# Sums of the first down-projection operands, formed by adding DMA transfers in memory instead of on VectorE

## The chip, the cores and the metric

The kernel runs on one core of one Trainium2 chip. The metric is the device time of one execution in microseconds, taken as the median of three runs.

## The reference, cut to what matters

The program is one decoder layer in float32: a mixer of two parts, an output projection, and then the channel mixer, which is where the change lies. For 512 rows of width 2048 it computes

```
h    = rmsnorm(x, norm2_g)
up   = h @ ffn_w_up                       # 2048 -> 2 * 6144
up   = causal depthwise conv, width 3, over rows
gate, val = split(up, 2)
x    = x + (gelu(gate) * val) @ ffn_w_down   # 6144 -> 2048
out  = rmsnorm(x, final_g)
```

The product `gelu(gate) * val` (512 rows by 6144 channels) is the left operand of the down projection.

## The kernel before, in words

**Fast block products.** Both big matrices of the channel mixer are multiplied by a Winograd scheme: two matrices of 2 by 2 blocks are multiplied with seven block products instead of eight. Each operand then needs, beside its four blocks, sums of its blocks. A tile `q` of eight slots of 128x256 holds one operand: slots 4 to 7 its four blocks as loaded, slots 0 to 3 the sums. The tables `SLOTS` and `ORDER` say which slots the seven products take and in which order they run. Float32 precision comes from splitting each slot into a rounded part (a cast on ScalarE, `h`) and a rest (a subtraction on VectorE, `l`; both at L126 and L127), and each product is three matmuls.

**Units and blocks.** The work goes through a stream of items: weight tiles (`Weights`) and operand tiles (`Acts`). A unit is one weight tile against one operand: 42 matmuls of 128x256. There are 24 blocks of 8 units for the up projection (unit numbers `u` 0 to 191; 12 groups `g`, each a gate block and a `val` block), and then three chunks of the down projection (units from 192; chunk 0 takes operands 0 to 7). Each item goes through `load` (a DMA on SP's queue into one of three rotating `q` buffers, a buffer being free again once its split is done), `sums` (three VectorE instructions, L646 to L648 for weights, L672 to L674 for operands; nothing where the sums were made beforehand) and `pair` (the split). The function `prepare` puts them in this order on the engines: the sums of item n+1, then the split of item n. All three engines run a fixed order from there on.

**Block ends.** The seven products of a block stand in seven of the eight PSUM banks. After a block VectorE and ScalarE combine them (`combine`, L870 to L878 in up blocks, L971 to L978 in down blocks), and TensorE takes over one bank after another as they come free. Later, spread over the steps of the next block, the convolution (`tap`, `rest`), gelu, and for `val` blocks the product with the gate (L921) follow. The product is written to memory by a POOL DMA, into `ad[p]`, 128 rows by 4 slots of 256 columns (L923). It is read back as an operand (L666) when its chunk begins.

**Sums made beforehand.** For the units around the start of each chunk (units 184 to 199 for chunk 0) the sums of the weights are made in memory: a list `to_make` of POOL transfers copies blocks and adds others (`accum_op`), and `make(n, after)` issues the next n of them. With `after` given, a one-column copy into `pace` (L318) holds POOL back until the last split of weights is done, so the list is spread over the whole program. These weights come with two loads, the sums (L639, 512 KB) and three of the blocks (L640, 384 KB).

The operands of chunk 0 cannot be split ahead: their tiles are the same as those of the up projection, so operand i waits until unit 184+i has been multiplied. They stand in the stream after the weights of units 187, 188, 190, 191, 193, 194, 196 and 197.

Of the kernel before, what the change touches and what calls it, by code (L numbers as in the profile page):

```python
# [8 lines left out]
F32 = mybir.dt.float32  # L9
# [3 lines left out]
ALU = mybir.AluOpType  # L13

P = 128
# [31 lines left out]
CHUNKS = [range(0, 8), range(8, 16), range(16, 22)]  # L47
# [31 lines left out]
def hybrid_block(ctx: ExitStack, tc: tile.TileContext, x, xT, w_in, w_out, w_up, w_dn, w_m4, w_dl, wab, wsT, vec, bs, vgb, fg, out):  # L79
    nc = tc.nc  # L80
# [213 lines left out]
    made = {}  # L294
# [13 lines left out]
    to_make = []  # L308
# [3 lines left out]
                to_make += copies[n] if part == 0 else added[n][0] if part == 1 else [added[n][1][part - 2]]  # L312
    pace = const.tile([P, 1], F32, name="pace")

    def make(n, after=None):

        if after is not None:
            nc.gpsimd.tensor_copy(pace, after)  # L318
        for _ in range(min(n, len(to_make))):
            add, dst, src = to_make.pop(0)  # L320
            how = {"accum_op": ALU.add} if add else {}
            nc.gpsimd.dma_start(dst, src, max_dma_last_dim=8192, **how)  # L322

# [192 lines left out]
    for i in range(2):  # L516
        for st in range(NS):
            t = vv[i][:, st]
# [5 lines left out]
    for i in range(2):  # L524
        ps = project(w_in, B_U + i, xg, True)
        t = rp.tile([P, 4, S], F32, name="uu", tag="r")
# [78 lines left out]
    x2d = [tc.dram_tile([P, NS, 512], F32, name=f"x2d{d}") for d in range(4)]  # L605
    ad = [tc.dram_tile([P, 4, 256], F32, name=f"ad{i}") for i in range(NP)]

    def squares2(d):
        nc.gpsimd.dma_start(x2d[d], x2[d])
        for st in range(NS):  # L610
            sq = pools["t"].tile([P, S], F32, name="sq", tag="sq", bufs=2)
            nc.scalar.activation(sq, x2[d][:, st], AF.Square, accum_out=ss2[:, st, d:d + 1])
# [15 lines left out]
    class Weights:  # L628


        def __init__(self, src, made=None):
            self.src, self.made = src, made
# [9 lines left out]
        def sums(self):  # L642
            q = self.q
            if self.made is not None:
                return
            nc.vector.tensor_tensor(q[:, 2:4], q[:, 5:7], q[:, 7:8].broadcast_to([P, 2, 256]), ALU.add)  # L646
            nc.vector.tensor_tensor(q[:, 1], q[:, 2], q[:, 6], ALU.add)
            nc.vector.tensor_tensor(q[:, 0], q[:, 1], q[:, 4], ALU.add)  # L648
# [8 lines left out]
    class Acts:  # L657


        def __init__(self, m, src=None, fill=None):  # L660
            self.m, self.src, self.fill = m, src, fill

        def load(self):
            self.q = slots("q")
            if self.fill is None:
                nc.sync.dma_start(self.q[:, 4:8], self.src)  # L666
            else:
                self.fill(self.q)

        def sums(self):  # L670
            q = self.q
            nc.vector.tensor_tensor(q[:, 2:4], q[:, 7:8].broadcast_to([P, 2, 256]), q[:, 5:7], ALU.subtract)  # L672
            nc.vector.tensor_tensor(q[:, 1], q[:, 6], q[:, 2], ALU.subtract)
            nc.vector.tensor_tensor(q[:, 0], q[:, 4], q[:, 1], ALU.subtract)  # L674
# [34 lines left out]
    def rest_of_loads():  # L709
        while halves:  # L710
            halves.pop(0)()
# [54 lines left out]
    spread = (0, 1, 3, 4, 6, 7, 9, 10)  # L766
    after = {}
    for m in range(8):
        after.setdefault(max(2, m), []).append(Acts(m, fill=from_rows(m)))
    for c, s in zip(CHUNKS, starts):  # L770
        for i, p in enumerate(c):
            after.setdefault(s - 8 + spread[i] + 3, []).append(Acts(i, src=ad[p]))

    def half_tiles(d):
        if d < 3:
# [82 lines left out]
    def later(step, f):  # L858
        lazy.setdefault(step, []).append(f)
# [22 lines left out]
    def up_block(g, val, u0):  # L882
        q = {}
        for m in range(8):
            prepare(ready(u0 + m))
            for p in ORDER:
                product(q, p, act[m], stream[place[u0 + m]].hl, True, m == 0, m == 7)
                if p == 6:
                    rest_of_loads()
            make(len(to_make) - n_make + n_make * (u0 + m + 1) // (n_up - 16), latest[0][:, 0, 0:1].bitcast(F32))  # L890
            if m == 7 and u0 == 0:
                pads[:] = [t_tile(f"pad{n}", [P, 2, S + 2]) for n in range(2)]
                for t in pads:
                    nc.gpsimd.memset(t[:, :, 0:2], 0.0)
            for f in lazy.pop(u0 + m, ()):
                f()
        c1 = t_tile("c1", [P, 2, 256])
        lo, hi = slice(2, 258), slice(258, 514)
        combine(q, c1, pads[0][:, :, lo], pads[1][:, :, lo], pads[0][:, :, hi], pads[1][:, :, hi])
        if u0 == 0:  # L900
            pools["ps"].release()
            pools["tr"].release()
            pools["ps"] = psum("q1", 8)

        def tap(n, j, f):
            if val:
                dst = t_tile("cv", [P, 2, S])if j == 0 else cvs[n]
                cvs[n] = dst
            else:
                if j == 0:  # L910
                    gates[n] = t_tile("gate", [P, 2, S], 2)
                dst = gates[n]
            nc.scalar.activation(dst[:, j], pads[n][:, j, 2:2 + S], AF.Identity, bias=col(V_FB + f), scale=col(V_FW + 2 * 96 + f))

        def rest(n, j, f):
            dst = (cvs if val else gates)[n][:, j]
            for i in (1, 0):
                nc.vector.scalar_tensor_tensor(dst, pads[n][:, j, i:i + S], col(V_FW + i * 96 + f), dst, ALU.mult, ALU.add)
            if val:
                gate = gates[n][:, j]  # L920
                nc.vector.tensor_tensor(gate, gate, dst, ALU.mult)  # L921
                at = 0 if j else 2
                nc.gpsimd.dma_start(ad[2 * g + n][:, at:at + 2], gate.rearrange("p (a b) -> p a b", a=2))  # L923

        def gelu(n, j):
            t = gates[n][:, j]
            nc.scalar.activation(t, t, AF.Gelu_apprx_tanh)

        cvs = {}
        at = u0 + 8  # L930
        for i, (n, j) in enumerate(((1, 0), (1, 1), (0, 0), (0, 1))):
            f = 48 * val + 4 * g + 2 * n + j
            step = at + (0, 1, 3, 4)[i]
            later(step, lambda n=n, j=j, f=f: tap(n, j, f))
            later(step + 1, lambda n=n, j=j, f=f: rest(n, j, f))
            if not val:
                later(step + 2, lambda n=n, j=j: gelu(n, j))

    pads = []
    for b, (g, val) in enumerate(ups):  # L940
# [6 lines left out]
    def down_block(ci, n, u0):  # L947
        tt = nc.vector.tensor_tensor
        size = len(CHUNKS[ci])
        q = {}  # L950
        for m in range(size):
            prepare(ready(u0 + m))
            if m == (6 if u0 == n_up else 1):
                if u0 == n_up:

                    pools["t"].release()
                    pools["x"] = pool("tx", "right")

            for half, at in ((0, 6 if u0 == n_up else 1), (1, 6 if u0 == n_up else 3)):
                if m == at:  # L960
                    t = pools["x"].tile([P, 2, 512], F32, name="xs", tag="xs", bufs=3)
                    nc.gpsimd.dma_start(t, x2d[n][:, 2 * half:2 * half + 2])
                    xs[n, half] = t
            for p in ORDER:
                product(q, p, act[m], stream[place[u0 + m]].hl, False, m == 0, m == size - 1)
            for f in lazy.pop(u0 + m, ()):
                f()
        X1, X2 = xs[n, 0], xs[n, 1]
        X11, X12, X21, X22 = X1[:, :, 0:256], X1[:, :, 256:512], X2[:, :, 0:256], X2[:, :, 256:512]
        c6, c5, c7 = (pools["x"].tile([P, 2, 256], F32, name="cc", tag="cc", bufs=3) for _ in range(3))  # L970
        tt(X11, X11, q[1], ALU.add)  # L971
        tt(X11, X11, q[2], ALU.add)  # L972
        nc.scalar.copy(c6, q[6])
        tt(c6, c6, q[1], ALU.subtract)
        nc.scalar.copy(c5, q[5])
        tt(X12, X12, q[3], ALU.add)
        nc.scalar.copy(c7, q[7])
        tt(X21, X21, q[4], ALU.add)  # L978
        steps = [
            lambda: tt(c5, c5, c6, ALU.add),  # L980
            lambda: tt(X12, X12, c5, ALU.add),
            lambda: tt(c6, c6, c7, ALU.add),
            lambda: tt(X21, X21, c6, ALU.subtract),
            lambda: tt(c5, c5, c7, ALU.add),
            lambda: tt(X22, X22, c5, ALU.add),
        ]
        if u0 + size == len(units):
            prepare(len(stream) - 2)
            for f in steps:
                f()  # L990
            prepare(len(stream) - 1)
            return
        at = u0 + size
        for i in range(3):
            later(at + i, steps[2 * i])
            later(at + i, steps[2 * i + 1])
        for half, t, step in ((0, X1, 0), (1, X2, 2)):
            later(at + step, lambda half=half, t=t: nc.gpsimd.dma_start(x2d[n][:, 2 * half:2 * half + 2], t))
# [6 lines left out]
    for n in DORD[:3]:  # L1005
        t = slots("q").rearrange("p a b -> p (a b)").rearrange("p (a b) -> p a b", a=NS)
# [116 lines left out]
```

## Time and profile before

| | us |
|---|---|
| median of 3 runs | 2063.87 (2063.66 to 2065.06) |
| the profiled execution | 2063.26 |
| its span in the trace | 2061.6 |
| TensorE busy | 2033.9 |
| VectorE busy | 1730.7 |
| ScalarE busy | 904.3 |
| POOL busy | 418.7 |

A row of groups names the line, the engine, the operation and its shapes, then the busy time, the mean duration in ns, and behind the second bar the idle time before these instructions with what ended it. A window row gives the busy time and the count of instructions of each engine in a stretch of time, then the granted TensorE clock (1.00 is full), the mean busy share of the 16 DMA engines and the GB/s moved. TensorE shows as busy for a matmul's whole modelled length, so a count of matmuls per stretch says more than its busy time.

### The profile page before, as it was taken

What the parts mean: (1) busy time and instruction counts of PE and PEld (TensorE: products, weight loads), DVE (VectorE), ACT (ScalarE), POOL (GpSimd) and SP (SyncE); (2) the same over time, 40 slices, a digit from 0 to 9 for tenths busy, and PEclk for the clock granted to TensorE, in tenths of its full rate; (3) what the DMA queues carried; (4) which work ended last, traced back from release to release, by engine and by line L of the source; (5) the groups of instructions that cost most, each with busy time, mean ns of one, the idle gap of its engine ahead of it and who ended that gap; (6) DMA issues with size and microseconds to landing.
All of it is one profiled execution on the core that took longest, in us unless ns stands there. A gap on an engine that the chain in (4) does not pass through costs nothing.

```text
span 2061.6 us, 35459 instructions
## 1 busy us (share of the span) xinstructions
PE 2033.9 (99%) x14528; PEld 1920.2 (93%) x14528; DVE 1730.7 (84%) x2183; ACT 904.3 (44%) x887; POOL 418.7 (20%) x702
## 2 busy tenths in 40 slices
PE   9999999999989999999999999999999999999998
PEld 7888888888889999999999999999999999999996
DVE  7598882644379999999999999999989979879986
ACT  6445322423274444444444444444455345445443
POOL 0332233211222222222222222222211000000001
PEclk9999999999999999999999999999999999999999
DMA  7666687666435566656555655565556568558573
GB/s 244 185 170 165 176 208 178 179 188 203 139 120 161 164 160 177 172 154 179 167 156 172 167 169 172 161 172 159 154 206 214 189 224 277 184 196 285 175 245 138
DMA packets 105907, 376.39 MB, mean 183 GB/s; under 512 B 14608, under 2 KB 22160, under 8 KB 91792
## 3 DMA queue, kind: packets, MB, share of 16 engines
q1 hardware_dynamic: 65808, 246.30, 35.5%
q0 software_dynamic: 39360, 127.17, 25.6%
q8 instruction: 113, 1.85, 0.4%
q10 hardware_dynamic: 576, 0.66, 0.1%
q14 instruction: 50, 0.41, 0.1%
HBM read 341.57 MB, written 110.36 MB: 219 GB/s over the span
## 4 chain that ended last, share of the span: by engine, by line
PE 93%; DVE 4%; DMA 1%; ACT 1%; issue 0%; SPq 0%; DVEq 0%; ACTq 0%
PE qs L854 64%; PE ps L162 9%; PE ps L164 9%; PE ps L163 9%; DVE wl L127 1%; DMA q<-ad 1%; PE qs L163 1%; PE qs L164 1%; PE qs L162 1%; DVE al L127 1%; PE tr L751 0%; PE ps L582 0%; ACT wh L126 0%; DVE q L672 0%; DMA wraw<-w_in 0%
## 5 line engine op out<-in xcount | busy, mean ns | idle before, releaser
L854 PE MATMUL qs<-ah,wh 128*128 128x256 f32 x2688 | 762.7, 284 | 2.1 <-DVE pad L871 1.8
L854 PE MATMUL qs<-al,wh 128*128 128x256 f32 x2688 | 761.5, 283 | 0.0
L854 PE MATMUL qs<-ah,wl 128*128 128x256 f32 x2688 | 761.5, 283 | 0.0
L126 ACT CAST wh<-q 128x1792 fp32r<-128x1792 f32 (+1 forms) x282 | 476.7, 1691 | 640.1 <-PE qs L854 459.6
L127 DVE TENSOR_TENSOR wl<-q,wh 128x1792 fp32r<-128x1792 f32 (+1 forms) x282 | 567.7, 2013 | 54.2 <-ACT wh L126 53.6
L854 PEld LDWEIGHTS qs<-ah,wh 128*128 128x128 f32 x2688 | 516.8, 192 | 2.5 <-DVE pad L871 2.0
L854 PEld LDWEIGHTS qs<-al,wh 128*128 128x128 f32 x2688 | 516.8, 192 | 0.2 <-DVE al L127 0.2
L854 PEld LDWEIGHTS qs<-ah,wl 128*128 128x128 f32 x2688 | 516.8, 192 | 0.0
L854 PE MATMUL qs<-wh,ah 128*128 128x256 f32 x1232 | 350.4, 284 | 5.7 <-DVE xs L972 2.6
L854 PE MATMUL qs<-wl,ah 128*128 128x256 f32 x1232 | 349.8, 284 | 0.0
L854 PE MATMUL qs<-wh,al 128*128 128x256 f32 x1232 | 349.7, 284 | 0.0
L318 POOL COPY pace<-wl 128x1 f32<-128x1 f32 x236 | 125.8, 533 | 975.5 <-DVE wl L127 965.5
L127 DVE TENSOR_TENSOR wl<-wraw,wh 128x1024 fp32r<-128x1024 f32 (+2 forms) x105 | 117.9, 1125 | 150.6 <-ACT wh L126 145.7
L854 PEld LDWEIGHTS qs<-wh,ah 128*128 128x128 f32 x1232 | 237.6, 193 | 6.9 <-DVE xs L972 3.0
L854 PEld LDWEIGHTS qs<-wl,ah 128*128 128x128 f32 x1232 | 237.6, 193 | 0.1
L854 PEld LDWEIGHTS qs<-wh,al 128*128 128x128 f32 x1232 | 237.6, 193 | 0.0
L322 POOL DMA_DIRECT2D made<-w_m x324 | 232.1, 842 | 15.8 <-issue 15.7
L126 ACT CAST wh<-wraw 128x1024 fp32r<-128x1024 f32 (+2 forms) x105 | 102.1, 974 | 274.6 <-PE ps L163 142.6
L646 DVE TENSOR_TENSOR q<-q 128x512 f32<-128x512 f32 x226 | 154.5, 684 | 2.7 <-DMA q<-w_dn 2.6
L162 PE MATMUL ps<-xgh,wh 128*128 128x512 f32 x384 | 152.1, 397 | 0.7 <-ACT wh L126 0.7
L163 PE MATMUL ps<-xgl,wh 128*128 128x512 f32 x384 | 151.6, 395 | 0.0
L164 PE MATMUL ps<-xgh,wl 128*128 128x512 f32 x384 | 150.0, 395 | 0.0
(242 smaller groups left out, 2499.4 us busy)
## 6 DMA issues: line engine op xcount, KB each, us to landing
q<-w_up SPq DMA_DIRECT2D x176, 512.0 KB, 3.5
made<-w_m POOLq DMA_DIRECT2D x270, 256.0 KB, 5.0
wraw<-w_in SPq DMA_DIRECT2D x28, 1024.0 KB, 6.1
q<-made SPq DMA_DIRECT2D x54, 512.0 KB, 3.7
q<-w_dn SPq DMA_DIRECT2D x50, 512.0 KB, 3.6
wraw<-w_out SPq DMA_DIRECT2D x16, 1024.0 KB, 6.1
q<-w_dn SPq DMA_DIRECT2D x38, 384.0 KB, 4.5
ad<-gate POOLq DMA_DIRECT2D x48, 256.0 KB, 3.5
```

Of the source, the lines that this page charges most:

```text
L126: nc.scalar.copy(h, src)
L127: nc.vector.tensor_tensor(l, src, h.bitcast(F32), ALU.subtract)
L162: nc.tensor.matmul(ps, lhsT=ah, rhs=bh, start=start, stop=False)
L163: nc.tensor.matmul(ps, lhsT=ah, rhs=bl, start=False, stop=False)
L164: nc.tensor.matmul(ps, lhsT=al, rhs=bh, start=False, stop=stop)
L318: nc.gpsimd.tensor_copy(pace, after)
L322: nc.gpsimd.dma_start(dst, src, max_dma_last_dim=8192, **how)
L646: nc.vector.tensor_tensor(q[:, 2:4], q[:, 5:7], q[:, 7:8].broadcast_to([P, 2, 256]), ALU.add)
L854: nc.tensor.matmul(q[p][:, t], lhsT=x_, rhs=y_, start=first and t == 0 and n == 0, stop=last and t == 1 and n == 2, skip_group_check=True)
```

## The change

It concerns the operands of chunk 0 alone. Their products are stored slot by slot (`ap[i]`, 4 slots of 128 rows by 256 columns), and in each of them two of the four quarter tiles with the opposite sign, so that all sums become plain additions. A second array `sums_of[i]` receives the four sums. They are made by five POOL transfers for each operand: two copies, then three that add. For these a slot is seen as 16 rows of 2048 elements (8 KB). One of the 40 transfers is issued at every second unit from unit 80 on (`make(1, todo=sum_up)`), with no pacing copy of its own. The operand is then loaded with two transfers (512 KB of sums, 384 KB of blocks) and has no sums on VectorE. The gate product is split into two halves of 256 columns, each with a factor of 1 or -1. In chunk 0 the combination after a down block subtracts where it added, since the products 2, 3, 5 and 7 now have the other sign.

```diff
@@ make @@
-    def make(n, after=None):
+    def make(n, after=None, todo=to_make):
...
-        for _ in range(min(n, len(to_make))):
-            add, dst, src = to_make.pop(0)
+        for _ in range(min(n, len(todo))):
+            add, dst, src = todo.pop(0)
@@ arrays in memory @@
+    ap, sums_of = ([tc.dram_tile([4, P, 256], F32, name=f"{n}{i}") for i in CHUNKS[0]] for n in ("ap", "as"))
+    for i in CHUNKS[0]:
+        ad[i] = ap[i].rearrange("s p c -> p s c")
@@ Acts.load, Acts.sums @@
+            if self.made is not None:
+                nc.sync.dma_start(self.q[:, 0:4], self.made.rearrange("s p c -> p s c"))
+                nc.sync.dma_start(self.q[:, 4:7], self.src[:, 0:3])
...
+            if self.made is not None:
+                return
@@ up_block @@
+            if u0 >= 80 and m % 2:
+                make(1, todo=sum_up)
             make(len(to_make) - n_make + n_make * (u0 + m + 1) // (n_up - 16), latest[0][:, 0, 0:1].bitcast(F32))
...
-                nc.vector.tensor_tensor(gate, gate, dst, ALU.mult)
+                if 2 * g + n in CHUNKS[0]:
+                    for t in (slice(0, 256), slice(256, 512)):
+                        nc.vector.scalar_tensor_tensor(gate[:, t], gate[:, t], -1.0 if (t.start == 0) == (j == 1) else 1.0, dst[:, t], ALU.mult, ALU.mult)
+                else:
+                    nc.vector.tensor_tensor(gate, gate, dst, ALU.mult)
@@ before the up blocks @@
+    sum_up = []
+    for k in range(len(CHUNKS[0]) + 3):
+        for r in range(4):
+            if 0 <= k - r < len(CHUNKS[0]):
+                dst, src = (t.rearrange("s (a b) c -> s a (b c)", b=8) for t in (sums_of[k - r], ap[k - r]))
+                sum_up += [
+                    [(0, dst[0:2], src[0:3:2]), (0, dst[2:4], src[1:3])],
+                    [(1, dst, src[3:4].broadcast_to([4, 16, 2048]))],
+                    [(1, dst[0:2], src[1:2].broadcast_to([2, 16, 2048]))],
+                    [(1, dst[0], src[2])],
+                ][r]
@@ down_block, likewise for X12, c5, c6 @@
+        plus = ALU.subtract if ci == 0 else ALU.add
-        tt(X11, X11, q[2], ALU.add)
+        tt(X11, X11, q[2], plus)
```

Three places show what moves. The first is POOL's queue around unit 93 in the difference of the two programs (`made` are the sums of weights, `as` the new sums, `ap` the slot-wise products; the shape is that of the transfer's list of rows, outermost count first).

```order
 L318 COPY pace<-wl 128x1
 L322 DMA made_596<-w_m 32x2048
+L322 DMA as_3713<-ap_3705 4x16x2048
 L318 COPY pace<-wl 128x1
 L322 DMA made_595<-w_m 32x2048
 L318 COPY pace<-wl 128x1
 L322 DMA made_595<-w_m 32x2048
+L322 DMA as_3715<-ap_3707 2x16x2048
 L318 COPY pace<-wl 128x1
 L322 DMA made_594<-w_m 128x512
```

A new transfer stands right behind a transfer of the old list, and the next `pace` copy behind it. Of the five for an operand three have an outermost count of 2 or 4 (one copy, two that add), the others 32 or 16 rows.

The second is VectorE's queue at the start of chunk 0 (units 186 to 188), before:

```order
L127 TENSOR_TENSOR wl<-q,wh 128x1792
L672 TENSOR_TENSOR q<-q 128x512
L673 TENSOR_TENSOR q<-q 128x256
L674 TENSOR_TENSOR q<-q 128x256
L127 TENSOR_TENSOR wl<-q,wh 128x1792
L127 TENSOR_TENSOR al_15210<-q,ah_15209 128x1792
L918 SCALAR_TENSOR_TENSOR gate<-pad_4967,vc,gate 128x512 x2
```

and now:

```order
L127 TENSOR_TENSOR wl<-q,wh 128x1792 x2
L127 TENSOR_TENSOR al_15280<-q,ah_15279 128x1792
L929 SCALAR_TENSOR_TENSOR gate<-pad_4983,vc,gate 128x512 x2
L127 TENSOR_TENSOR wl<-q,wh 128x1792
L127 TENSOR_TENSOR al_15340<-q,ah_15339 128x1792
```

The three sums of an operand are gone, so the split of the weights before it no longer stands behind the operand's load.

The third is SP's queue there, before:

```order
L666 DMA q<-ad_3682 128x1024
L639 DMA q<-made_569 128x1024
L640 DMA q<-w_up 128x768
L639 DMA q<-made_570 128x1024
L640 DMA q<-w_up 128x768
```

and now:

```order
L670 DMA q<-as_3714 128x4x256
L671 DMA q<-ap_3706 128x3x256
L643 DMA q<-made_569 128x1024
L644 DMA q<-w_up 128x768
L643 DMA q<-made_570 128x1024
```

An operand's load has become two transfers with rows of 1 KB in place of one with rows of 4 KB.

More of the change, by code (lines that the diff above doesn't have):

```diff
@@ L657, in hybrid_block, with __init__ @@
     class Acts:
-        def __init__(self, m, src=None, fill=None):
-            self.m, self.src, self.fill = m, src, fill
+        def __init__(self, m, src=None, fill=None, made=None):
+            self.m, self.src, self.fill, self.made = m, src, fill, made
         def load(self):
             self.q = slots("q")
-            if self.fill is None:
+            if self.made is not None:
+                nc.sync.dma_start(self.q[:, 0:4], self.made.rearrange("s p c -> p s c"))
+                nc.sync.dma_start(self.q[:, 4:7], self.src[:, 0:3])
+            elif self.fill is None:
                 nc.sync.dma_start(self.q[:, 4:8], self.src)
@@ L771, in hybrid_block @@
         for i, p in enumerate(c):
-            after.setdefault(s - 8 + spread[i] + 3, []).append(Acts(i, src=ad[p]))
+            after.setdefault(s - 8 + spread[i] + 3, []).append(Acts(i, src=ad[p], made=sums_of[i] if c is CHUNKS[0] else None))
     def half_tiles(d):
@@ L975, in down_block @@
         nc.scalar.copy(c5, q[5])
-        tt(X12, X12, q[3], ALU.add)
+        tt(X12, X12, q[3], plus)
         nc.scalar.copy(c7, q[7])
@@ L979, in down_block @@
         steps = [
-            lambda: tt(c5, c5, c6, ALU.add),
+            lambda: tt(c5, c6, c5, plus),
             lambda: tt(X12, X12, c5, ALU.add),
-            lambda: tt(c6, c6, c7, ALU.add),
+            lambda: tt(c6, c6, c7, plus),
             lambda: tt(X21, X21, c6, ALU.subtract),
-            lambda: tt(c5, c5, c7, ALU.add),
+            lambda: tt(c5, c5, c7, plus),
             lambda: tt(X22, X22, c5, ALU.add),
```

## The prediction

> **What bounds the kernel now.** I read the page first, then the groups and waits of TensorE, then the windows around unit 192, then VectorE's order in the up projection, and last the DMA queues.
>
> ```profile
> span 2061.6 us, 35459 instructions
> PE 2033.9 (99%) x14528; PEld 1920.2 (93%) x14528; DVE 1730.7 (84%) x2183; ACT 904.3 (44%) x887; POOL 418.7 (20%) x702
> ```
>
> TensorE bounds it. In the up projection (620 to 1510 us) it hardly ever waits, as the groups of its instructions there show:
>
> ```profile
> L854 PE MATMUL qs<-ah,wh 128*128 128x256 f32 x2465 | 697.8, 283 | 2.1 <-DVE pad L871 1.8 <-DVE v L877 0.3
> ```
>
> The windows around the start of chunk 0 show where it does wait (columns: stretch; PE, PEld, DVE, ACT, POOL; clock; DMA share; GB/s), and its timeline names the two waits:
>
> ```profile
> 1540.00:1550.00 10.00, 10.00 (x86) 10.00 (x85) 9.90 (x10) 6.99 (x6) 2.82 (x2) 1.00 0.53 186
> 1550.00:1560.00 10.00, 7.60 (x59) 7.40 (x59) 9.01 (x9) 6.38 (x6) 2.28 (x3) 0.92 0.68 244
> 1560.00:1570.00 10.00, 9.39 (x61) 9.09 (x61) 9.62 (x13) 3.60 (x4) 0.63 (x1) 0.74 0.40 141
> 1600.00:1610.00 10.00, 8.41 (x67) 7.90 (x67) 9.76 (x14) 4.86 (x5) 0.55 (x2) 1.00 0.83 291
> ...
> 1558.98 0.58 PE L854 MATMUL qs<-wh,ah 128*128 128x256 f32 x1 [2.40 <-ACT c L870]
> 1561.24 0.58 PE L854 MATMUL qs<-wh,ah 128*128 128x256 f32 x1 [0.61 <-DVE pad L871]
> ```
>
> Full pace is 85.5 recorded matmuls in 10 us. The three short windows lack 26.5 + 24.5 + 18.5 = 69.5, or 8.1 us. That is all there is to win here. About 3 us of it is no wait but a lower clock behind the wait (61 matmuls at a clock of 0.74 with only 0.61 us idle).
>
> The cause is VectorE: before the banks of the last up block are freed (L871) stand five operands' sums, and they wait for loads.
>
> ```profile
> 1518.92 2.02 DVE L127 TENSOR_TENSOR wl<-q,wh 128x1792 fp32r<-128x1792 f32 x1
> ...
> 1560.51 0.68 DVE L871 TENSOR_TENSOR pad<-c,qs 128x512 f32<-128x512 f32 x1
> ...
> L672 DVE TENSOR_TENSOR q<-q 128x512 f32<-128x512 f32 x8 | 5.5, 688 | 3.0 <-DMA q<-ad 3.0
> L674 DVE TENSOR_TENSOR q<-q 128x256 f32<-128x256 f32 x8 | 3.4, 425 | 0.3
> ```
>
> **What the change removes at chunk 0.** Per operand 0.69 + 0.43 + 0.43 = 1.54 us of VectorE, eight times 12.3 us. Five operands stand before L871: 7.7 us, and with the 3.0 us of waits at most 10.7 us. By VectorE alone L871 could start at 1550. The three `q` buffers allow less. A buffer's turn is the load, the cast, the split. An operand's load now looks like that of made weights, whose second transfer is issued 0.37 us after the first and lands as SP's rows say:
>
> ```profile
> 1509.26 0.33 SPq L639 DMA_DIRECT2D q<-made  x1
> 1509.63 0.43 SPq L640 DMA_DIRECT2D q<-w_up  x1
> ...
> DMA to landing us min/median/max: 4.0/4.2/5.4
> ...
> 1558.82 1.69 ACT L126 CAST wh<-q 128x1792 fp32r<-128x1792 f32 x1
> ```
>
> A turn is 0.4 + 4.2 + 1.7 + 2.0 + 0.2 for handing over = 8.5 us, with the longest landing 9.7; with the added traffic I take 9.0. From the split that ends at 1520.9 four turns lead to the split before L871: 1520.9 + 36 = 1556.9 instead of 1560.5. TensorE then waits about 1 us instead of 3.0, too little to expect the slow stretch (3 us); the wait of 1600 to 1610 (18.5 matmuls, 2.2 us) loses three more operands' sums, and I count half. Gain 2 + 3 + 1 = **6 us** (bounds 0 and 8.1).
>
> **Gate products.** Sixteen instructions of 128x512 become 32 of 128x256, in four `val` blocks.
>
> ```profile
> L921 DVE TENSOR_TENSOR gate<-gate,cv 128x512 f32<-128x512 f32 x20 | 13.8, 692 | 0.7
> L647 DVE TENSOR_TENSOR q<-q 128x256 f32<-128x256 f32 x79 | 33.6, 425 | 2.7
> L646 DVE TENSOR_TENSOR q<-q 128x512 f32<-128x512 f32 x79 | 54.0, 684 | 0.0
> L918 DVE SCALAR_TENSOR_TENSOR gate<-pad,vc,gate 128x512 f32<-128x512 f32 x40 | 29.9, 749 | 0.7
> ```
>
> Two at 0.425 are 0.16 us more than one at 0.692; with the 0.065 by which the scaled form is dearer at 512 columns (749 against 684) 0.29 us. Four of them in two blocks: 0.6 to 1.2 us. VectorE has just that much room, one wait of 1.19 us in every two blocks:
>
> ```profile
> DVE wl L127 <- ACT wh L126: 13.3, 11, 1.5
> ...
> 1031.17 0.68 DVE L871 TENSOR_TENSOR pad<-c,qs 128x512 f32<-128x512 f32 x1
> ...
> 1068.73 2.03 DVE L127 TENSOR_TENSOR wl<-q,wh 128x1792 fp32r<-128x1792 f32 x1 [1.19 <-ACT wh L126]
> ...
> 1111.80 0.68 DVE L871 TENSOR_TENSOR pad<-c,qs 128x512 f32<-128x512 f32 x1
> ```
>
> From L871 to L871 two blocks last 80.63 us. I count 0.5 us for all; without that cover it is 4 x 1.2 = 4.8.
>
> **The forty transfers.** POOL's groups from 1000 to 1400 us, and the landing of the old transfers:
>
> ```profile
> L322 POOL DMA_DIRECT2D made<-w_m x81 | 57.0, 711 | 4.1 <-issue 4.1
> L318 POOL COPY pace<-wl 128x1 f32<-128x1 f32 x79 | 39.5, 500 | 264.2 <-DVE wl L127 264.2
> ...
> made<-w_m POOLq DMA_DIRECT2D x270, 256.0 KB, 5.0
> ```
>
> On POOL the new ones cost nothing: 40 x 0.7 = 28 us of issue against 264 us in which `pace` waits for VectorE. Behind them in POOL's queue stand the next `pace` copy, the next old transfer and the stores of the gate products, for which nothing waits before the next chunk. What counts is the loads of weights beside them, since VectorE has 1.19 us to lose in 80. A load is issued when a split ends, lands 3.5 us later (row below, SP's L637 from 1000 to 1400 us), and its sums stand at a fixed place in VectorE's order:
>
> ```profile
> 1037.47 2.02 DVE L127 TENSOR_TENSOR wl<-q,wh 128x1792 fp32r<-128x1792 f32 x1
> ...
> 1044.31 0.69 DVE L646 TENSOR_TENSOR q<-q 128x512 f32<-128x512 f32 x1
> ...
> 1064.00 2.02 DVE L127 TENSOR_TENSOR wl<-q,wh 128x1792 fp32r<-128x1792 f32 x1
> ...
> 1075.45 0.68 DVE L646 TENSOR_TENSOR q<-q 128x512 f32<-128x512 f32 x1
> ...
> DMA to landing us min/median/max: 3.3/3.5/5.8
> ```
>
> In the first pair the split ends at 1039.4 and the sums of the load issued then begin at 1044.3: 4.9 us, 1.4 us of room. In the second it is 1065.9 to 1075.45, 9.5 us. Of the sixteen loads of two blocks four have 4.9 us, four 5.6, two 6.3 and six 7.8 to 9.5.
>
> The price of a row comes from the DMA view of two windows in which one old transfer of 32 rows of 8 KB runs (its 48 packets are 32 rows and 16 short marks): 1050 to 1053.2 us, an adding one, and 1063 to 1065, a copy (the first line is the first window in 40 slices, in tenths):
>
> ```profile
> DMA  6989796959892990009949400050559000000000
> q0 software_dynamic: 48, 0.26, 45.2%
> ...
> q0 software_dynamic: 47, 0.26, 31.9%
> ```
>
> 45.2% of 16 engines over 3.2 us is 23.1 us, 0.72 us for an added row; 31.9% over 2 us is 10.2 us, 0.33 for a copied one. At first all engines are busy (the digits of 9): the 32 rows are dealt two to an engine.
>
> How a transfer with an outermost count of 2 or 4 is dealt, no row shows; every one of before has 32 or 128. Bounds: by rows over 16 engines (4 added rows each for the 512 KB one), or by its outermost pieces over 4 or 2 engines, 16 rows each. The old ones fit both, as there a piece is a row. I take the pieces, 7 to 3, because they are what the transfer's list names first. [...]
>
> With pieces an adding transfer holds its engines 16 x 0.72 = 11.5 us. A load of 512 KB gives every engine 8 rows of 4 KB. If each waits behind one added row, it lands 8 x 0.72 = 5.8 us late, after 9.3 us. Against the room that is late by 4.4 (four loads), 3.7 (four), 3.0 (two) and about 0.8 (six), 2.7 in the mean. Loads come 3.4 to 8.2 us apart, so each adding transfer meets one nearly whole; but some of its rows have gone before the load comes, and 0.72 holds some waiting of its own. I take 2.0: 16 x 2.0 = 32 us. The eight uneven copies (8 x 0.33 = 2.6 us late) cost 1 us. Behind the late sums stand the split, the next sums and at a block's end the evacuation, and TensorE waits for that. VectorE gives back its 1.19 us in each of the five double blocks that the transfers span (40 x 10.1 us): 6 us, and evacuations can be 1 us late. Left are 32 + 1 - 6 - 1 = **26 us** (bounds 0, and 16 x 4.4 - 6 = 64).
>
> Each block's end in that stretch then has a wait of about 2.6 us, like the one of 2.40 above that brought a lower clock. A slowed TensorE lets VectorE catch up, so I count 2 us in all.
>
> **Sum.** The profiled execution took 2063.26, its span 2061.6; the runs' median is 2063.87, so the same. 2063.3 - 6 + 0.5 + 26 + 2 = **2086 us**.
>
> **Rivals.**
>
> *Spread over all engines, faster.* Then an adding transfer of 512 KB puts 4 rows, 2.9 us, on each engine, the others no more than the old ones do, beside which a load took up to 5.8 us and TensorE never waited. A load lands after 6.4 us, late by 1.5 for four in sixteen and 0.8 for four, 0.6 in the mean; eight of these, 4.8 us, are less than the 6 us given back. 2063.3 - 6 + 0.5 = 2058. It decides where a hit costs a load under about 2 us. For it: the digits of 9. Against: the outermost counts.
>
> *Spread, but the buffers take the gain, no change.* The operands' loads bring 384 KB more and rows of 1 KB into a stretch where DMA already stands at 0.68 to 0.83. If a turn takes 9.9 us, L871 comes at 1560.5 as now; only the 1 us of the later wait is left and the gate products take half: 2063.
>
> *Every wait slows the clock.* If each of ten block ends pays 3 us of lower clock, with nothing caught up, it is 2086 - 2 + 30 = 2114. For it: the clock of 0.74 after a wait of 2.4 us. [...]
>
> That the sums come too late for their loads I exclude: the last transfer stands near unit 160, the first load behind unit 185.
>
> **How the numbers follow.** The forecast has 0.62, the clock rival 0.08, the faster one 0.18, no change 0.12. About 0.2% (4 us) is what a measurement here can tell from no change: faster 0.18, same 0.12, slower 0.70. If pieces are right, the range by itself is 2068 to 2108 (a mean lateness of 0.9 to 3.4 us). To leave out no more than 2 in 10 it has to reach the faster case too: 2058 to 2108.
>
> **What would show it.** The transfers of 2x16x2048 and 4x16x2048 would land after 10 us and more, where the old ones took 5; loads of weights between 990 and 1400 us would land after up to 9 us; VectorE would wait there for q<-w_up, some 30 us in all; TensorE would wait at the ends of those ten blocks. From 1550 to 1610 us' counterpart the counts should be near 85. If the loads keep 3.5 us with a longest near 6, the step on the engines is wrong, and the time is near 2058.

## The result, and the profile after

The change makes the kernel slower: 2121.67 us median of four runs (2120.86 to 2123.78) against 2064.47 before, also of four (2063.66 to 2065.28), a ratio of 1.0280 with a 95% interval of 1.0267 to 1.0293. The profiled execution took 2123.78, its span 2122.1. That is 36 us over the forecast and 14 over the end of its range.

The page, then the DMA issues of the kernel after (size, median us from issue to landing), which answer to the 5.0 us of the old transfers and the 3.5 us of the loads:

```profile
span 2122.1 us, 35510 instructions
PE 2049.7 (97%) x14528; PEld 1930.8 (91%) x14528; DVE 1723.6 (81%) x2175; ACT 905.2 (43%) x887; POOL 443.7 (21%) x742
...
PE 71%; DVE 14%; DMA 11%; ACT 2%; issue 2%; SPq 0%; DVEq 0%; ACTq 0%
...
made<-w_m POOLq DMA_DIRECT2D x270, 256.0 KB, 5.1
...
as<-ap POOLq DMA_DIRECT2D x24, 256.0 KB, 10.0
...
as<-ap POOLq DMA_DIRECT2D x8, 512.0 KB, 16.1
```

VectorE is no longer busier, it has 7 us less work, and yet 14% of the chain of what ended last is its own and 11% is DMA. The new transfers take two to three times as long as the old ones of 256 KB (the 10.0 is the median of copies, of adds on two engines and of eight even copies). The waits of VectorE, of TensorE between 980 and 1580 us, and the loads of weights (SP's L641, 980 to 1480 us) tell the rest (columns of the waits: us in total, times, longest):

```profile
DVE q L650 <- DMA q<-w_up: 65.2, 21, 6.5
...
PE qs L863 <- DVE pad L880: 27.8, 9, 8.1
PE qs L863 <- DVE wl L127: 13.8, 8, 3.3
...
  DVE q L650: 64.9, 20
...
DMA to landing us min/median/max: 3.3/4.7/11.8
```

Where the time is lost is read from the evacuation that ends a block (L871 before, L880 after; L971 and L1002 in the first down block). Before:

```profile
990.03 0.68 DVE L871 TENSOR_TENSOR pad<-c,qs 128x512 f32<-128x512 f32 x1
...
1514.14 0.68 DVE L871 TENSOR_TENSOR pad<-c,qs 128x512 f32<-128x512 f32 x1
...
1605.48 0.68 DVE L971 TENSOR_TENSOR xs<-xs,qs 128x512 f32<-128x512 f32 x1
```

and after:

```profile
992.44 0.68 DVE L880 TENSOR_TENSOR pad<-c,qs 128x512 f32<-128x512 f32 x1
...
1576.98 0.68 DVE L880 TENSOR_TENSOR pad<-c,qs 128x512 f32<-128x512 f32 x1
1621.66 0.68 DVE L880 TENSOR_TENSOR pad<-c,qs 128x512 f32<-128x512 f32 x1
1664.27 0.69 DVE L1002 TENSOR_TENSOR xs<-xs,qs 128x512 f32<-128x512 f32 x1
```

The stretch in which the transfers are issued takes 584.54 us in place of 524.11, **60.4 us more**. The transition to chunk 0 behind it takes 87.29 in place of 91.34, **4.05 us less**. The difference of the spans, 60.5, is these two, 2.4 us that were there at 992 already, and 1.7 behind. The 2.4 us need not be the change's: the first evacuation of the up projection, ahead of all that the edits move, comes anywhere from 626.4 to 631.0 us in the traces of the kernels of this document.

VectorE's 64.9 us of waits for weights are 4.5 more than that: so much of its room it gave back, as I read it. TensorE pays partly in waits (41.6 us in the two rows above) and partly in a lower clock, as the windows of the kernel after show (columns as in the prediction):

```profile
640.00:1000.00 360.00, 360.00 (x3003) 360.00 (x3002) 345.17 (x452) 163.49 (x136) 95.12 (x159) 1.00 0.60 166
...
1100.00:1480.00 380.00, 342.27 (x2735) 338.52 (x2734) 318.74 (x402) 150.91 (x124) 109.97 (x180) 0.96 0.64 169
```

### The profile page after: what moved, and what is told of

Same layout as the page of the kernel before. It is cut to its first block, busy times and chain, and to the rows that moved or that the text cites. A ratio compares the mean times of both kernels' runs of the same rounds, so it can differ in the third digit from the quotient of the medians.

```text
span 2122.1 us, 35510 instructions
## 1 busy us (share of the span) xinstructions
PE 2049.7 (97%) x14528; PEld 1930.8 (91%) x14528; DVE 1723.6 (81%) x2175; ACT 905.2 (43%) x887; POOL 443.7 (21%) x742
## 4 chain that ended last, share of the span: by engine, by line
PE 71%; DVE 14%; DMA 11%; ACT 2%; issue 2%; SPq 0%; DVEq 0%; ACTq 0%
PE qs L863 42%; DMA q<-w_up 9%; PE ps L162 8%; PE ps L164 8%; PE ps L163 8%; DVE wl L127 7%; DVE q L650 2%; DVE q L651 1%; ACT wh L126 1%; DVE al L127 1%; PE qs L163 1%; PE qs L164 1%; PE qs L162 1%; DMA q<-w_dn 1%; DVE gate L929 1%
## 5 line engine op out<-in xcount | busy, mean ns | idle before, releaser
L318 POOL COPY pace<-wl 128x1 f32<-128x1 f32 x236 | 115.6, 490 | 1000.3 <-DVE wl L127 990.4
L650 DVE TENSOR_TENSOR q<-q 128x512 f32<-128x512 f32 x226 | 154.9, 685 | 67.8 <-DMA q<-w_up 65.2
```

## The experiments

The kernels were run in three sets, each on one chip beside the kernel before: e1 to e4 beside 2065.71 us (15 runs), e5 to e8 beside 2065.70 (21), e9 to e12 beside 2064.87 (21). "Waits" is VectorE's wait for `q<-w_up` in the profile; the last column is how long the 512 KB adding transfers took to land.

| run | transfers | us | ratio (95% interval) | waits, us | 512 KB lands, us |
|---|---|---|---|---|---|
| the change | 24 on few engines | 2121.67 | 1.0280 (1.0267 to 1.0293) | 65.2 | 16.1 |
| e1_spread | all spread | 2066.93 | 1.0005 (0.9996 to 1.0013) | 4.5 | 7.3 |
| e2_add4 | eight 512 KB adds on few | 2099.33 | 1.0166 (1.0150 to 1.0181) | 38.0 | 15.9 |
| e3_add2 | eight 256 KB adds on few | 2098.18 | 1.0157 (1.0144 to 1.0171) | 40.9 | 7.1 |
| e4_copy2 | eight copies on few | 2078.22 | 1.0060 (1.0046 to 1.0073) | 17.9 | 7.1 |
| e5_rows4k | as e2, rows of 4 KB | 2087.75 | 1.0109 (1.0093 to 1.0124) | 28.9 | 17.1 |
| e9_rows2k | as e2, rows of 2 KB | 2083.76 | 1.0091 (1.0077 to 1.0104) | 25.9 | 17.5 |
| e6_none | none | 2061.53 | 0.9981 (0.9972 to 0.9990) | 0.2 | |
| e8_transfers_only | all spread, unused | 2073.52 | 1.0043 (1.0030 to 1.0055) | 6.9 | 7.9 |
| e10_roomy_narrow | the change's, other units | 2101.34 | 1.0176 (1.0162 to 1.0189) | 37.8 | 15.5 |
| e7_roomy | all spread, other units | 2062.39 | 0.9984 (0.9975 to 0.9993) | 0.4 | 7.4 |
| e11_roomy_again | the same | 2061.59 | 0.9986 (0.9977 to 0.9995) | 1.1 | 7.2 |
| e12_spread_again | as e1 | 2066.87 | 1.0006 (0.9997 to 1.0015) | 5.5 | 7.2 |

### Is it the few engines?

Theory 1: the transfers with an outermost count of 2 or 4 lie on 2 or 4 engines, and the loads of weights wait there. The rival: 11.5 MB (8 x 1408 KB) more of traffic beside the loads costs it, however it is dealt. The edit puts the 16 rows outermost; by theory 1 the same rows of 8 KB then go over 16 engines:

```diff
-                dst, src = (t.rearrange("s (a b) c -> s a (b c)", b=8) for t in (sums_of[k - r], ap[k - r]))
+                dst, src = (t.rearrange("s (a b) c -> a s (b c)", b=8) for t in (sums_of[k - r], ap[k - r]))
...
-                    [(1, dst, src[3:4].broadcast_to([4, 16, 2048]))],
+                    [(1, dst, src[:, 3:4].broadcast_to([16, 4, 2048]))],
```

> The same forty transfers with the same bytes and the same 8 KB rows, but with the 16 rows of a slot outermost (16x4x2048 and 16x2x2048 instead of 4x16x2048 and 2x16x2048). Theory 1, few engines: the transfers of the changed kernel ran on 4 or 2 engines; now each puts 4 or 2 rows on all 16, lands after 5 to 7 us instead of 10 to 16, loads of weights land within 6.5 us, VectorE waits for q<-w_up at most 6 us in all (65.2 in the changed kernel), and the time is 2058 to 2062. Rival, the adding traffic itself (its bytes in memory, its issues on POOL): nothing changes, 2110 to 2122.

The DMA issues, VectorE's wait and the landing of the loads of weights in e1_spread:

```profile
as<-ap POOLq DMA_DIRECT2D x24, 256.0 KB, 5.4
...
as<-ap POOLq DMA_DIRECT2D x8, 512.0 KB, 7.3
...
DVE q L650 <- DMA q<-w_up: 4.5, 7, 1.1
...
DMA to landing us min/median/max: 3.4/3.6/8.6
```

2066.93 us, 5 above the range that I had expected, and the latest load landed after 8.6 us, not 6.5. But with the 16 rows outermost the 256 KB transfers land like the old ones (5.4 and 5.1 us), the 512 KB ones after 7.3 us in place of 16.1, and 55 of the 57 us are gone; the traffic is the same. The rival falls. How many engines an uneven transfer holds is seen in windows of the change in which only the added rows and the rows of a load are at work: behind a 512 KB adding transfer, from 1087.5 to 1090.7 us, both queues come to 4.0 engines (19.6% and 5.4% of 16), behind a 256 KB one, from 1323.1 to 1324.7 us, to 2.0 (9.8% and 2.7%). That the spread ones lie on all 16 is read from their landings; no window here counts them.

### Which transfers pay, and how much?

Here the two theories of the price are: (1a) each uneven transfer pays by itself, and the prediction's price was too low; (1b) two of them in flight at once pay for each other. Each run takes e1_spread and puts one kind alone back on few engines (for e2_add4 this is the line; the other two do the same with the adding `dst[0:2]` and with the copy `dst[:, 0:2]`):

```diff
-                    [(1, dst, src[:, 3:4].broadcast_to([16, 4, 2048]))],
+                    [(1, ndst, nsrc[3:4].broadcast_to([4, 16, 2048]))],
```

> Only the eight adding transfers of 512 KB keep their outermost count of 4; the other 32 have 16 or 32 outermost. In the changed kernel VectorE waited 64.9 us for loads of weights in this stretch, about 57 of it behind the sixteen uneven adding transfers, 3.6 each. Theory 1a, each transfer pays by itself and the forecast only had the price of one too low: 29 us of such waits here, 6 of them covered, 2082. Theory 1b, two uneven transfers in flight together make the price: 2.0 each as forecast, 16 us of waits, 2069.

> Only the eight adding transfers of 256 KB keep their outermost count of 2. They have as many rows per engine (16) as those of 512 KB, on half as many engines. Theory 1a: 29 us of waits, 2082, the same as with the 512 KB ones, since a load is as late as its latest engine. Theory 1b: 16 us, 2069. If the share of the engines counted and not the latest one, about half of what the 512 KB ones cost.

> Only the eight copies of 256 KB keep their outermost count of 2. A copied row took 0.33 us where an added one took 0.72. Theory 1a: 7 us of waits as behind these copies in the changed kernel (0.9 each), all but 1 covered by the room VectorE has: 2059 to 2062. Theory 1b: less than 7 us, the same time. If the price of a row did not matter, only that few engines are held: 29 us, 2082.

VectorE's wait in the three, in the order e2, e3, e4:

```profile
DVE q L650 <- DMA q<-w_up: 38.0, 11, 5.9
```

```profile
DVE q L650 <- DMA q<-w_up: 40.9, 16, 6.0
```

```profile
DVE q L650 <- DMA q<-w_up: 17.9, 12, 3.1
```

Alone, the 512 KB ones cost 38.0 / 8 = 4.75 us each, the 256 KB ones 5.1, the copies 2.2. e1_spread, where no transfer is uneven, has 4.5 us of such waits too; less these the copies cost 1.7. So 1b falls: each pays by itself, and more than the 3.6 of 1a (29 us and 2082 expected; 38.0 and 40.9 us, 2099.33 and 2098.18 measured). The 512 KB and the 256 KB ones, on 4.0 and 2.0 engines by the windows of the change, cost about the same, and in the change the 256 KB adding ones land after 14.1 to 15.9 us, the 512 KB ones after 15.0 to 17.0: what they share is 16 added rows on an engine, 32 over 2 and 64 over 4. That the latest engine decides is the reading of this, not more. The copies, too, cost more than 1a expected (17.9 us for 7). And the three do not add up: 96.8 us alone, in which those 4.5 us can stand three times, 65.2 together.

### How a load waits

The prediction let each of a load's eight rows on such an engine wait behind one added row, and one load pay for a transfer. A new theory then was that the load waits until the rest of the transfer has gone. Cutting the rows tells them apart, since the engine has about the same 10 us of rows to do, 16 x 0.63, 32 x 0.33 or 64 x 0.17 us by the windows below (e5_rows4k; e9_rows2k has 2048 and `[4, 64, 512]`):

```diff
-            nc.gpsimd.dma_start(dst, src, max_dma_last_dim=8192, **how)
+            nc.gpsimd.dma_start(dst, src, max_dma_last_dim=4096 if add == 2 else 8192, **how)
...
-                    [(1, ndst, nsrc[3:4].broadcast_to([4, 16, 2048]))],
+                    [(2, ndst, nsrc[3:4].broadcast_to([4, 32, 1024]))],
```

> The run with only the eight 512 KB adding transfers on few engines, again, but with their rows cut to 4 KB (four pieces of 32 rows instead of 16 rows of 8 KB). Theory of the prediction's working (a row of a load waits behind one row of the adding transfer at a time, by turns): a wait is half as long, so the loads of weights land at most about 8 to 9 us after their issue, VectorE waits about 15 us or less for them, and the time is near 2078 us. New theory (a load's rows on such an engine wait until most of what is left of the adding transfer's rows has gone): cutting the rows changes nothing but their number, the longest landing stays near 12 us, VectorE waits 35 to 45 us, and the time is 2095 to 2105 us.

> The eight 512 KB adding transfers on few engines once more, their rows cut to 2 KB (four pieces of 64 rows; an engine still has some 10 us of added rows to do). Theory now: on such an engine the rows of a load and of the adding transfer take turns one by one, and what a load is late by is handed to the next load on that engine if its rows are not done when that comes. With 2 KB rows a load's eight rows pass such an engine in about 8 x (0.16 + 0.16) = 2.6 us, less than the 5 us between loads, so nothing is handed on: a load lands about 1.3 us late, VectorE waits 5 to 14 us for weights, and the time is 2066 to 2074 us. If a load has to wait for most of the remaining rows, however short, VectorE waits 35 us and more and the time is near 2097. If only the sum of the added rows' time counts, it is that of the 4 KB rows: waits near 29 us, time near 2088.

The waits were 28.9 and 25.9 us, the times 2087.75 and 2083.76: in between, and both of my expectations for a theory alone missed. "Only the sum of the added rows' time counts" came nearest. The DMA view shows what happens on the engines while only these two queues are at work (POOL's q0 with the added rows, SP's q1 with the load's; packets, MB, share of 16 engines). In e5_rows4k, three half microseconds in a row from 1079.5 to 1081:

```profile
q0 software_dynamic: 4, 0.02, 16.4%
q1 hardware_dynamic: 4, 0.02, 8.7%
...
q0 software_dynamic: 4, 0.02, 16.4%
q1 hardware_dynamic: 4, 0.02, 8.7%
...
q0 software_dynamic: 4, 0.02, 16.4%
q1 hardware_dynamic: 4, 0.02, 8.7%
```

25.1% of 16 engines is 4.0 engines, and on each one added row of 0.33 us and one load row of 0.17 us pass per half microsecond: they take turns, one by one. With 8 KB rows (e2_add4, 1057 to 1061 us) and 2 KB rows (e9_rows2k, 1079.5 to 1081 us):

```profile
DMA packets 53, 0.26 MB, mean 65 GB/s; under 512 B 8, under 2 KB 8, under 8 KB 35
...
q0 software_dynamic: 26, 0.15, 17.8%
q1 hardware_dynamic: 27, 0.11, 7.1%
```

```profile
q0 software_dynamic: 20, 0.04, 14.0%
q1 hardware_dynamic: 17, 0.07, 12.3%
```

In e2 the 26 hold 8 short marks: 18 added rows of 0.63 us beside 27 load rows, again 4.0 engines. In e9 20 of 0.17 us beside 17. In the change, with 8 KB rows and nothing else on the engines, it is 16 beside 16 from 1087.5 to 1090.7 us, and 4 beside 4 on the two engines from 1323.1 to 1324.7 us, where the slices of 0.04 us show the order as well, an added row starting at each 9 and a load row at each 2:

```profile
DMA  0900000200090000200009000020000900002000
...
q0 software_dynamic: 4, 0.03, 9.8%
q1 hardware_dynamic: 4, 0.02, 2.7%
```

Eight load rows to an engine is an estimate, a load's 128 rows over 16; in the kernel before, load rows alone keep 82.8% of 16 engines busy from 1067 to 1068 us. With one added row before each of the eight, and the rows' times above, a load would be 5.0 us late with 8 KB rows, 2.6 with 4 KB, 1.4 with 2 KB: with 8 KB near the 5.8 that the prediction took.

What a transfer costs VectorE is seen in VectorE's order. One transfer, issued at 1043.18 in e2_add4 and at 1040.17 in e5_rows4k, is followed by these sums of weights. e2_add4, behind the loads' rows of SP's L641:

```profile
L641 SPq DMA_DIRECT2D q<-w_up x91: 327/328/328, 983.5 to 1474.1; - x91
...
DMA to landing us min/median/max: 3.4/3.8/11.9
...
1048.45 2.02 DVE L127 TENSOR_TENSOR wl<-q,wh 128x1792 fp32r<-128x1792 f32 x1
...
1056.81 0.69 DVE L650 TENSOR_TENSOR q<-q 128x512 f32<-128x512 f32 x1 [4.89 <-DMA q<-w_up]
...
1062.39 0.69 DVE L650 TENSOR_TENSOR q<-q 128x512 f32<-128x512 f32 x1 [2.04 <-DMA q<-w_up]
```

and e5_rows4k:

```profile
1051.67 0.69 DVE L650 TENSOR_TENSOR q<-q 128x512 f32<-128x512 f32 x1 [2.77 <-DMA q<-w_up]
1055.81 0.69 DVE L650 TENSOR_TENSOR q<-q 128x512 f32<-128x512 f32 x1 [0.58 <-DMA q<-w_up]
1062.31 0.69 DVE L650 TENSOR_TENSOR q<-q 128x512 f32<-128x512 f32 x1 [1.50 <-DMA q<-w_up]
```

The change has such a pair too (4.76 and 2.08 us, before L650 at 1059.41 and 1065.03). The landings of the three loads behind the transfer at 1043.18 in e2_add4, issued near 1045, 1050 and 1060 us:

```profile
q<-w_up SPq DMA_DIRECT2D x1, 512.0 KB, 11.2
...
q<-w_up SPq DMA_DIRECT2D x1, 512.0 KB, 11.9
...
q<-w_up SPq DMA_DIRECT2D x1, 512.0 KB, 4.9
```

For all eight 512 KB transfers of each run, read off the DMA view in the same way:

| run | first load lands, us | second | third | first wait behind each, of all waits, us |
|---|---|---|---|---|
| e2_add4, 8 KB rows | 10.5 to 11.9 | 6.9 to 11.9 | 3.5 to 6.2 | 35.0 of 38.0 |
| e5_rows4k | 8.2 to 9.3 | 7.4 to 8.8 | 7.0 to 8.8 | 15.4 of 28.9 |
| e9_rows2k | 7.3 to 8.5 | 6.5 to 7.8 | 6.7 to 8.3 | 16.4 of 25.9 |

So with 8 KB rows nearly all of the price is one wait, 4.4 us in the mean, for the first load, which is 7.0 to 8.4 us late against the usual 3.5. The second load lands late as well, but VectorE, late by then, hardly waits for it. The 1043.18 transfer, whose second wait is 2.04 us, is the exception. With shorter rows the first load is less late, but three loads in a row are late and more of the waits fall on the later ones. And in all three runs the first load is later than the turns of rows give, by 2.0 to 3.4, 2.1 to 3.2 and 2.4 to 3.6 us, whatever the length of a row. Both together are, as I read it, why shorter rows help little. What that constant part is stays open. The old adding transfers before and behind the new one in POOL's queue may be in it; the view counts all engines together and does not tell them apart.

### What the transfers and the transition are worth apart

The next two take e1_spread and the kernel before and leave out one side each: the transfers (e6_none, which loads the operand's blocks where the sums belong, so its output is not the reference's), or their use (e8_transfers_only).

```diff
@@ e6_none, from e1_spread @@
-                nc.sync.dma_start(self.q[:, 0:4], self.made.rearrange("s p c -> p s c"))
+                nc.sync.dma_start(self.q[:, 0:4], self.src)
...
-                sum_up += [
@@ e8_transfers_only, from before @@
+            if u0 >= 80 and m % 2:
+                make(1, todo=sum_up)
...
+                nc.vector.tensor_tensor(q[:, 2:4], q[:, 5:7], q[:, 7:8].broadcast_to([P, 2, 256]), ALU.add)
```

> The change without its 40 transfers; the operand's first four slots are loaded, in the same rows of 1 KB and from the blocks in memory, without their sums (left out: the sums of the first chunk's operands, so the output is not the reference's). It shows what the gate products and the transition to the first chunk are worth by themselves. If the spread transfers cost nothing when timed, it takes the time of the run with all transfers spread, 2064 to 2068 us. If these cost some 6 us that the one profiled execution did not show, it takes 2058 to 2061 us.

> The kernel before with the first chunk's blocks stored by slots and signed, its sums made on VectorE from the loaded operand as before, and the 40 spread transfers beside it, whose results nobody reads. It tells the transfers' own cost from the gain of doing without VectorE's sums. If spread transfers are free, it takes the time of the kernel before, 2063 to 2067 us; if they cost some 6 us, 2068 to 2073 us.

Without transfers the change takes 2061.53, 4.2 us under before: that is the transition's gain with the gate products in it. The spread transfers take 5.4 us back (2066.93 in e1, though in another set). Beside VectorE's sums the kernel is 7.8 us slower than before, somewhat more than expected (2073.52). That is not the transfers' price alone: VectorE waits for operands as well, whose blocks now come in rows of 1 KB, 6.4 us where the kernel before had 3.0:

```profile
DVE q L650 <- DMA q<-w_up: 6.9, 5, 3.0
DVE q L677 <- DMA q<-ap: 6.4, 5, 2.4
```

So the spread transfers are not free either. By an estimate the 64 added rows of a 512 KB one, four to each of 16 engines, hold them for 4 x 0.63 = 2.5 us, more than the least room of a load, 1.4 us.

### Issuing behind the loads with room

In the prediction's rows four in sixteen loads have 4.9 us from the split to the sums, six 7.8 to 9.5. The next edit issues the transfers only behind units whose next load has most room, from unit 64 on; e7_roomy with the spread transfers, e10_roomy_narrow with those of the change.

```diff
-            if u0 >= 80 and m % 2:
+            if u0 >= 64 and m in ((6, 7) if u0 // 8 % 2 else (1, 4, 6, 7)):
```

> All transfers spread over the engines, and issued only behind units whose next load of weights has the most room before it is needed, from unit 64 on. If the spread transfers' cost is the 4.5 us of VectorE's waits for weights, these go to under 1.5 us and the time is 2058 to 2062 us, below the kernel before. If it is the bytes in memory or their number that costs, it stays at 2064 to 2068 us.

> The change itself with its transfers on few engines, but issued behind the units whose next load has the most room, as in the run that did that with spread transfers. Theory now (lateness is handed on over the three loads that meet a transfer in flight): room at the first of them hides little, VectorE still waits 40 to 65 us for weights, and the time is 2100 to 2122 us. If only the first load behind an issue pays, the waits fall under 25 us and the time is under 2085.

> The spread transfers behind the units with room, once more, beside the next run on the same chip: 2060 to 2064 us, and 0.1 to 0.25% under the kernel before, if the gain is one that lasts; else within 0.05% of it.

> The spread transfers behind every second unit from 80 on, once more: 3 to 6 us above the run with room and within 0.1% of the kernel before, if the units behind which the transfers are issued make that difference; the same as the run with room, if they do not.

e7 takes 2062.39 us and its repeat 2061.59, in both sets faster than before by 0.14 to 0.16%, less than the 0.2% that I had set as the least to tell, but twice with an interval that excludes no change; the spread transfers at the change's units take 2066.87 beside it, no faster than before. Of the 7.8 us between the two profiled executions, 4.8 were there before 990 us and tell nothing of the issue points; 2.9 come in the stretch (527.1 us) and 1.0 in the transition, and 0.9 are made up behind. The version with room beats both kernels, within 1 us of having no transfers at all. In e11_roomy_again the stretch lasts as long as before (524.2 us) and the transition 87.0:

```profile
989.49 0.68 DVE L880 TENSOR_TENSOR pad<-c,qs 128x512 f32<-128x512 f32 x1
...
1513.70 0.68 DVE L880 TENSOR_TENSOR pad<-c,qs 128x512 f32<-128x512 f32 x1
1557.50 0.68 DVE L880 TENSOR_TENSOR pad<-c,qs 128x512 f32<-128x512 f32 x1
1600.74 0.68 DVE L1002 TENSOR_TENSOR xs<-xs,qs 128x512 f32<-128x512 f32 x1
```

With few engines room helps only in part: 2101.34 us, as expected, and 37.8 us of waits in place of 65.2, a little under the 40 that I had expected at least. That fits a first load 7.0 to 8.4 us late, which is more than the most room, 9.5 - 3.5 = 6.0.

## Why the prediction was wrong in size and right in kind

**The engines: right.** The 7 to 3 for outermost pieces held, with 4.0 and 2.0 engines in the windows of the change, and the landings of 10 us and more (10.0 and 16.1 in the median) with it.

**The late loads: the step that failed.** The sum had 32 us for sixteen adding transfers, 2.0 each, from "If each waits behind one added row, it lands 8 x 0.72 = 5.8 us late" and "each adding transfer meets one nearly whole", cut down to 2.0 because some rows have gone before. The runs showed 4.75 to 5.1 us for each alone. The row's price was near (0.63 us in place of 0.72), and so were the turns, 5.0 us in place of 5.8. But the one load that the sum counted lands after 10.5 to 11.9 us in e2_add4 (10.8 to 11.5 in the change), not after 9.3: 2.0 to 3.4 us on top of the turns, whose source is open. By the prediction's own rooms a load 7.7 us late, the mean of the eight, waits some 4.5 us beyond them, an estimate; measured are 35.0 / 8 = 4.4. The cut from 2.7 to 2.0, for rows that would be gone before, went the wrong way. Later loads, which the sum left out, added 2.9 us to the 35.0. So the steps from transfer to engines to late load to wait were right, and the lateness of that load was the term set too low. The eight copies, set at 1 us in all, cost 17.9 by themselves, with the 4.5 of e1_spread in it. Together all 24 made VectorE wait 64.9 us, less than the 96.8 of the three kinds alone, because a VectorE that is late by one transfer asks later for the next load; that reason is argued, not measured. The bound of 64 us for this term was right, but I left the range's end at 0.9 to 3.4 us per transfer.

**What VectorE gives back:** 4.5 us for an expected 6 plus 1, 2.5 too many.

**The gate products:** nothing in place of 0.5 us. Two halves take 0.76 us together, where one whole took 0.69 and I reckoned with 0.98:

```profile
940.05 0.76 DVE L935 SCALAR_TENSOR_TENSOR gate<-gate,cv 128x256 f32<-128x256 f32 x2
```

The window of 640 to 1000 us above, with the blocks that have them, runs at the pace of the kernel before in 360 us without a wait:

```profile
1040.00:1400.00 360.00, 360.00 (x3002) 360.00 (x3002) 344.48 (x439) 163.00 (x137) 92.95 (x161) 1.00 0.59 167
```

3002 recorded matmuls there, 3003 here.

**The gain at chunk 0:** 4.05 us in place of 6. The evacuation before the first down block comes 44.68 us behind the one before it where it took 46.37 and I expected 42.8. The step on the buffers was too hopeful. An operand's second transfer lands after this, not after 4.2, which the turn of 9.0 still had room for:

```profile
DMA to landing us min/median/max: 4.5/4.7/6.0
```

But on the path to that evacuation the four turns, from 1584.1 us on, took 8.4, 10.0, 10.0 and 9.1 us. In the two of 10.0 the second transfer landed after 5.5 and 5.8 us.

The later wait gave more than the half I counted: 42.61 us to L1002 where it was 44.97 to L971.

**The clock:** I counted 2 us. A clock of 0.96 over 380 us is some 15 us, but I read it as no term of its own, since VectorE's waits less what it gives back already make up the stretch; no run takes the clock apart from the waits. The clock rival (2114) was near in time for another reason; its price was to come on top of the late loads. The waits at block ends were 3.1 us in the mean (27.8 / 9) and up to 8.1; from what length a wait lowers the clock was not shown.

**The rivals on spread rows:** their condition was not met by the change, and e1_spread shows what they would have been worth: 2066.93 us (2066.87 again), 0.05% over before. So the faster one (2058) was wrong also where its condition holds. It took 4.8 us of late loads to be covered by the room given back; the runs without transfers and with other issue points, 4 to 5 us shorter, say that they are not. The one of no change would have had the right time there by luck: the buffers did not take the gain, which is 4.2 us in e6_none; the transfers took it back.

## What to carry to other kernels

Write a transfer's shape so that its outermost count is 16 or 32, as in e1_spread; rows that are as long and as many, but behind an outermost count of 2 or 4, cost this kernel 55 us. Price a transfer that lies on few engines by the measured landing of the load that meets it, less that load's room; the turns of rows alone came out 2 to 3.6 us too low here, and shorter rows took off a third at most. Where a load feeds an engine without slack, put background transfers behind the loads whose data are needed last (2061.59 against 2066.87 us here).

## What I had not expected of the hardware

- The adding transfers of 64 rows on four engines and of 32 rows on two, 16 rows on an engine in both, cost about the same, 4.75 and 5.1 us: in these two runs it did not matter how many engines were held.
- Rows a quarter as long take a third off the waits, no more (38.0, 28.9, 25.9 us for 8, 4 and 2 KB). An added row of 4 or 2 KB takes 0.33 and 0.17 us, in proportion to its bytes, and where the windows show them alone, load rows and added rows pass about one by one.
- The profiled execution of e1_spread took 2060.19 us and its ten timed ones 2066.02 to 2068.93. In that execution VectorE waits 4.5 us. The same kernel in e12_spread_again was profiled at 2067.83, with 5.5 us of such waits; of the 7.6 us between the two spans 3.0 are there at the first evacuation of the up projection (627.98 against 631.01), 1.9 come in the stretch of the transfers and 1.4 in the transition. Why an execution is 3 us later before that was not found.
